# Equal start addresses modulo 512 bytes for every tile that TensorE reads

## The chip, the cores and the metric

The kernel runs on one NeuronCore of a Trainium2 chip. The metric is the device time of one execution in microseconds (us). All arrays are float32. Matrix products are made in float32 with three products per pair of operands (below), so TensorE does three times the work of the plain formula.

## The reference, cut to what matters

One encoder layer with shared weights, applied to a prompt of 256 tokens and a sample of 1024 tokens, width 1024:

```python
def encoder_layer(x, mem, ...):
    h = rmsnorm(x, g_mix_pre)
    z = h @ w_in                                     # 1024 -> 9216 columns
    rq, rk, rv, rg, pin, mq, gl = jnp.split(z, ...)
    gates = jax.nn.sigmoid(gl).reshape(b, s, 3, 1024)
    y_ret = retention_branch(rq, rk, rv, rg, ...) @ w_ret_out   # 4 heads, both directions, chunks
    y_pool = pool_branch(pin, pool_w, pool_scale) @ w_pool_out
    y_mem = memory_branch(mq, mem, g_mem, w_mem_kv) @ w_mem_out # 256 memory tokens, softmax
    merged = gates[:, :, 0] * y_ret + gates[:, :, 1] * y_pool + gates[:, :, 2] * y_mem
    x = x + rmsnorm(merged @ w_o, g_mix_post)
    h2 = rmsnorm(x, g_ffn_pre)
    u = conv3(h2 @ w_up)                             # 1024 -> 2 * 2816, depthwise conv of width 3
    gate, val = jnp.split(u, 2, axis=-1)
    return x + rmsnorm((gelu(gate) * val) @ w_down, g_ffn_post)
```

## The kernel before

**Work and order.** Tokens of both groups lie side by side (T = 1280). Each operand of a product is split by `hilo` (L136) into a rounded high part (ScalarE, L138 or L141) and the rest (VectorE, L139 or L142), and `mm3` (L145 to L148) makes three matmuls of them into one PSUM bank: high by high (L146), high by low (L147), low by high (L148). The order on every engine is that of the code; nothing reorders it. The stages follow each other: memory keys and values, queries of the memory branch and retention values, the pooling branch with the rotary products, the retention gate with the state chain, the gates with the retention chain, the three output projections, the output product with `w_o`, the feed-forward up product in 22 units with the convolution, and the down product in two halves of 640 tokens.

**What a matmul reads.** Each matmul instruction loads its own stationary operand (128 columns, 512 bytes in each partition; row "LDWEIGHTS" of the profile, engine PEld) and then streams its moving operand of 512 or 256 columns (2048 or 1024 bytes). The load of the next matmul starts while the matmul before it streams. So at any time two places in SBUF are read: the moving tile of the current matmul and the stationary tile of the next.

**Where the tiles lie.** Pools are laid out by hand-chosen order, from the left end of SBUF and, for the weight ring, from the right end.
- `wh` and `wl` (L79, L80): the split weights, four buffers of 4096 bytes each, at the right end.
- `b` (slots of `big`, L121 to L134): eight buffers of `SLOT` = 2·2·642 elements = 10272 bytes = 20·512 + 32, from the left. They hold the split activations hT, the operands of the output projections, five half-terms each of the up product (`hterm`, L1166), and at the end raw down-product input.
- `hc` (L1257): a tile at the right side below the ring, for the last 16 of the 56 half-terms (products B22 and T4).
- `h2p` (L1248): split prompt tokens of the up product, moving operand with 256 columns. `gl` (L1592): split down-product input, stationary. `lh` (L1145): stationary in the `w_o` product. `bx` (L974): two more slots at the right.
- `khl`, `qhl`, `vhl`, `pt` (memory branch), `k1hl`, `v1hl` (states), `qkvhl`, `sthl`, `shl` (retention), `memT` (memory), `pwh`, `dh` (pooling).

In the built program before, the start addresses modulo 512 are: `wh`, `wl` and `hc` 480; the eight buffers of `b` 192, 224, 256, 288, 320, 352, 384, 416; `bx` 416 and 448; `lh` 416; `gl` 256; `h2p` 128; `memT`, `khl`, `qhl`, `vhl`, `k1hl`, `v1hl`, `qkvhl`, `sthl` 128; `pt` 256; `shl` 352; `pwh` 0; `dh` 192 and 320; `ident` 128. Slices that a matmul takes of a tile start at multiples of 512 bytes from the tile's start, except in `dh`.

**The up product** of one unit q (a block of 128 gate columns and 128 value columns) has seven products of 12 matmuls with 512 columns, for the sample (`product`, L1305, matmul at L1309): B11, B21, T2, T1, T3 read half-terms in `b`; B22 and T4 read half-terms in `hc`. All seven take their stationary operand from `wh` and `wl`. Between them stand four groups of 12 matmuls with 256 columns for the prompt (`prompt`, L1312), whose moving operand is `h2p`.

**Small statistics.** Row sums, maxima and reciprocal square roots are tiles of 4 to 64 bytes, allocated in the pool of the stage that uses them.

Of the kernel before, what the change touches and what calls it, by code (L numbers as in the profile page):

```python
# [8 lines left out]
F32 = mybir.dt.float32  # L9
# [3 lines left out]
ALU = mybir.AluOpType  # L13
# [4 lines left out]
P = 128  # L18
# [3 lines left out]
T = TP + TS  # L22
KC = D // P
NT = T // P
H = 4
HD = 256
# [9 lines left out]
PAD = 16  # L36
PW = PAD + TP + PAD + TS + PAD
PCOLS = PW - 2 * PAD
SLOT = 2 * 2 * 642

PK = {}
_o = 0
# [67 lines left out]
def encoder(ctx: ExitStack, tc: tile.TileContext, a: dict):  # L110
    nc = tc.nc

    const = ctx.enter_context(tc.tile_pool(name="const", bufs=1))
    dram = ctx.enter_context(tc.tile_pool(name="scratch", bufs=1, space=DRAM))
    wpool = ctx.enter_context(tc.tile_pool(name="w", bufs=1, side="right"))
    big = ctx.enter_context(tc.tile_pool(name="big", bufs=1))
    ctx.enter_context(tc.manual_schedule())
# [46 lines left out]

    def rsqrt_act(pool, v, between=None):
        s = pool.tile([P, 1], F32, tag="rqs", name="rqs")
        y = pool.tile([P, 1], F32, tag="rqy", name="rqy", bufs=2)
        t = pool.tile([P, 1], F32, tag="rqt", name="rqt")
        nc.scalar.activation(s, v, AF.Sqrt)
        if between:  # L170
            between()
        nc.vector.reciprocal(out=y, in_=s[:])
        nc.vector.tensor_tensor(out=t, in0=y[:], in1=y[:], op=ALU.mult)
        nc.vector.scalar_tensor_tensor(out=t, in0=t[:], scalar=-0.5, in1=v, op0=ALU.mult, op1=ALU.mult)
        nc.vector.scalar_tensor_tensor(out=y, in0=t[:], scalar=1.5, in1=y[:], op0=ALU.add, op1=ALU.mult)
        return y
# [34 lines left out]
    nc.scalar.activation(warm, ident[:, 0:1], AF.Exp)  # L211
    pk = const.tile([P, PK_W], F32, name="pk")
    kc = const.tile([P, KC_W], F32, name="kc")

    def col(name, i=0, n=1):
        o, _ = PK[name]
# [69 lines left out]
    dec = ds.enter_context(tc.tile_pool(name="dec", bufs=1))  # L286
# [17 lines left out]
    b = chb(512)  # L304
# [81 lines left out]
            if c not in (4, 6):  # L386
                yield

    lg = dec.tile([P, 2 * H], F32, name="lg")
    kdec = dec.tile([P, 2, H, 2], F32, name="kdec")  # L390
    qdec = dec.tile([P, 2, H, 2], F32, name="qdec")
    cdec = dec.tile([P, 2 * H], F32, name="cdec")
    dtab = dec.tile([P, H, 2, C], F32, name="dtab")

    def decay_tables():
        d = col("decay_fwd", 0, 2 * H)
        u, s, s2, r = (s0.tile([P, 2 * H], F32, name=f"lg{i}") for i in range(4))
        nc.vector.tensor_scalar(out=u, in0=d, scalar1=-1.0, scalar2=None, op0=ALU.mult)
        nc.vector.tensor_tensor(out=u, in0=u[:], in1=d, op=ALU.min)
        nc.scalar.activation(u, u[:], AF.Exp)  # L400
        nc.vector.tensor_scalar(out=s, in0=u[:], scalar1=2.0, scalar2=None, op0=ALU.add)
        nc.vector.reciprocal(out=s, in_=s[:])
        nc.vector.tensor_tensor(out=s, in0=s[:], in1=u[:], op=ALU.mult)
        nc.vector.tensor_tensor(out=s2, in0=s[:], in1=s[:], op=ALU.mult)
        nc.vector.tensor_scalar(out=r, in0=s2[:], scalar1=2.0 / 19, scalar2=2.0 / 17, op0=ALU.mult, op1=ALU.add)
        for k in range(7, -1, -1):
            nc.vector.tensor_tensor(out=r, in0=r[:], in1=s2[:], op=ALU.mult)
            nc.vector.tensor_scalar(out=r, in0=r[:], scalar1=2.0 / (2 * k + 1), scalar2=None, op0=ALU.add)
        nc.vector.tensor_tensor(out=r, in0=r[:], in1=s[:], op=ALU.mult)
        nc.vector.tensor_scalar(out=u, in0=d, scalar1=0.0, scalar2=None, op0=ALU.min)  # L410
        nc.vector.tensor_tensor(out=lg, in0=u[:], in1=r[:], op=ALU.subtract)
        yield
        nc.scalar.activation(cdec, lg[:], AF.Exp, scale=float(C))
        for h in range(H):
            for dr in range(2):
                sc = lg[:, dr * H + h:dr * H + h + 1]
                nc.scalar.activation(qdec[:, dr, h, :], kcol("cmi" if dr else "ip1"), AF.Exp, scale=sc)
                nc.scalar.activation(kdec[:, dr, h, :], kcol("j" if dr else "cm1j"), AF.Exp, scale=sc)
        kd = kdec[:].rearrange("p a b c -> p (a b c)")
        nc.vector.tensor_scalar(out=kd, in0=kd, scalar1=HD ** -0.5, scalar2=None, op0=ALU.mult)  # L420
        yield
        rel = s0.tile([P, 2, 2 * C], F32, name="rel")
        nc.sync.dma_start(out=rel, in_=a["rel"])
        for h in range(H):
            dt = dtab[:, h].rearrange("p a b -> p (a b)")
            nc.vector.tensor_scalar(out=dt, in0=rel[:, 0, :], scalar1=lg[:, h:h + 1], scalar2=None, op0=ALU.mult)
            nc.vector.scalar_tensor_tensor(out=dt, in0=rel[:, 1, :], scalar=lg[:, H + h:H + h + 1], in1=dt,
                                           op0=ALU.mult, op1=ALU.add)
            nc.scalar.activation(dt, dt, AF.Exp)
            nc.vector.tensor_scalar(out=dt, in0=dt, scalar1=HD ** -0.5, scalar2=None, op0=ALU.mult)  # L430
            yield
# [67 lines left out]
    def mem_chain():  # L499
# [28 lines left out]
        def scores(n):  # L528
            h, j = jobs[n]
            q, k, mo = qs.pop(n), khl[h], (MEM if j else 0)  # L530
            b = chb(2, MEM)
            for i in range(2):
                for d in range(2):
                    ts = slice(i * P, (i + 1) * P)
                    mm3(b[:, i, :], q[:, 0, d, ts], q[:, 1, d, ts],
                        k[:, 0, d, mo:mo + MEM], k[:, 1, d, mo:mo + MEM], d == 0, d == 1)
            mx = mp.tile([P, 2], F32, tag="mx", name="mx", bufs=2)
            sm = mp.tile([P, 2], F32, tag="sm", name="sm", bufs=2)
            e = pr[n] = mp.tile([P, 2, MEM], F32, tag="pr", name="pr", bufs=2)
            nc.vector.tensor_reduce(out=mx, in_=b, axis=AX.X, op=ALU.max)  # L540
            nc.vector.tensor_scalar(out=mx, in0=mx[:], scalar1=-(HD ** -0.5), scalar2=None, op0=ALU.mult)
            for i in range(2):
                nc.scalar.activation(e[:, i, :], b[:, i, :], AF.Exp, scale=HD ** -0.5, bias=mx[:, i:i + 1],
                                     accum_out=sm[:, i:i + 1])
            nc.vector.reciprocal(out=sm, in_=sm[:])
            for i in range(2):
                nc.vector.tensor_scalar(out=e[:, i, :], in0=e[:, i, :], scalar1=sm[:, i:i + 1], scalar2=None,
                                        op0=ALU.mult)
# [34 lines left out]
        t = 0  # L583
# [249 lines left out]
    def ret_chain(rp):  # L833
# [51 lines left out]
        def output(n):  # L885
# [10 lines left out]
            if drs:  # L896
# [4 lines left out]
                for i in range(2):  # L901
# [5 lines left out]
                    for dr in drs:  # L907
                        nc.vector.scalar_tensor_tensor(out=y[:, i, :], in0=b[:, dr - lo, :],
                                                       scalar=qdec[:, dr, h, i:i + 1], in1=y[:, i, :],
                                                       op0=ALU.mult, op1=ALU.add)  # L910
            bs = rp.tile([P, 2, 6], F32, tag="bs", name="bs")
            ag = rp.tile([P, 2, 2], F32, tag="ag", name="ag")
            for i in range(2):
                nc.vector.bn_stats(out=bs[:, i, :], in_=src[:, i, :])
                nc.vector.bn_aggr(out=ag[:, i, :], in_=bs[:, i, :])
            rs = rsqrt(rp, ag[:, :, 1], 2, 1.0)
            for i in range(2):
                nc.vector.tensor_scalar(out=y[:, i, :], in0=src[:, i, :], scalar1=ag[:, i, 0:1],
                                        scalar2=rs[:, i:i + 1], op0=ALU.subtract, op1=ALU.mult)
# [182 lines left out]
    def finish(t, bs, x, bank):  # L1102
        u = xtile()
        v = xtile()
        ss = op.tile([P, 3], F32, tag="ss", name="ss", bufs=2)
        for i in range(2):
            nc.vector.tensor_tensor(out=u[:, i * 512:(i + 1) * 512], in0=bs[i], in1=gpost[:, i * 512:(i + 1) * 512],
                                    op=ALU.mult)
# [1 line left out]
        yield  # L1110
        nc.vector.scalar_tensor_tensor(out=ss[:, 0:1], in0=ss[:, 0:1], scalar=EPS, in1=ss[:, 1:2],
                                       op0=ALU.add, op1=ALU.add)
        rs = rsqrt_act(op, ss[:, 0:1])
        yield
        nc.vector.scalar_tensor_tensor(out=x, in0=u[:], scalar=rs[:, 0:1], in1=x[:], op0=ALU.mult, op1=ALU.add)
        nc.gpsimd.dma_start(out=x2_d[t][:], in_=x[:])
# [1 line left out]
        nc.scalar.activation(v, x[:], AF.Square, scale=D ** -0.5, accum_out=ss[:, 2:3])  # L1118
        yield
        nc.vector.tensor_scalar(out=ss[:, 2:3], in0=ss[:, 2:3], scalar1=EPS, scalar2=None, op0=ALU.add)  # L1120
        r2 = rsqrt_act(op, ss[:, 2:3])
        yield
        nc.vector.tensor_scalar(out=v, in0=x[:], scalar1=r2[:, 0:1], scalar2=None, op0=ALU.mult)
        yield
# [429 lines left out]
    def last_gain(i, hf, b, res):  # L1554
        cs = slice(hf * 512, (hf + 1) * 512)
        nc.vector.tensor_tensor(out=res[i][:, cs], in0=b, in1=gpost2[0][:, cs], op=ALU.mult)
# [27 lines left out]
    for hb in range(2):  # L1584
# [20 lines left out]
                g_split(k)  # L1605
        if hb == 0:
            gpost2.append(gain(a["g_ffn_post"]))
        ss = fp.tile([P, 2, 5], F32, tag="fss", name="fss", bufs=2)
        res = [fp.tile([P, D], F32, tag=f"res{i}", name="res") for i in range(5)]
        bs = [fbank()[:] for _ in range(5)]  # L1610
        held = []
# [34 lines left out]
        for i in range(5):  # L1646
            for n, w in held:
                partial(i, n, w)
            last_half(i, 1, bs[i], res, ss)
            if not hb:  # L1650
                last_gain(i, 1, bs[i], res)
            else:
                v = ss[:, 0, i:i + 1]
                nc.vector.scalar_tensor_tensor(out=v, in0=v, scalar=EPS, in1=ss[:, 1, i:i + 1],
                                               op0=ALU.add, op1=ALU.add)
                rs = rsqrt_act(fp, v, lambda: last_gain(i, 1, bs[i], res))
                close_tile(5 + i, res[i], rs[:, 0:1], xs.pop(0))
                if i + 3 < 5:
                    xs.append(load_x2(5 + i + 3))
# [83 lines left out]
```

## Time and profile before

| what | value |
|---|---|
| time, median of 3 runs | 2740.58 us (2740.44 to 2741.98) |
| profiled execution, its own time | 2741.42 us |
| its span in the profile | 2739.7 us |
| TensorE busy | 2683.1 us, 98% of the span |
| VectorE, ScalarE, GpSimd busy | 50%, 33%, 10% of the span |
| share of TensorE in the chain that ended last | 92% |
| granted TensorE clock, mean | 0.992 of full speed |

A matmul's own duration in the profile overlaps with the next one's. What a matmul costs is the time from its start to the start of the next; a run of equal matmuls gives it as the time from the first start to the start of what follows, divided by their number.

### The profile page before, as it was taken

The numbers are of one execution on the slowest core, as the hardware profiler recorded it, in microseconds if no ns is written. First come the engines' busy times: TensorE is split into PE (matmuls) and PEld (weight loads), VectorE is DVE, ScalarE is ACT, GpSimd is POOL, SyncE is SP. The second block draws the span as 40 slices with busy tenths as digits, with TensorE's granted clock in tenths as the row PEclk, the third lists the DMA queues.
The fourth block names the chain that finished last, engine by engine and source line by source line (L and its number), as shares of the span: only waits on it lengthen the run. The fifth ranks groups of instructions, "written<-read, shape, count | busy, mean of one in ns | idle before, by whom it ended". The sixth has DMA issues, their size and how long they took to land.

```text
span 2739.7 us, 36294 instructions
## 1 busy us (share of the span) xinstructions
PE 2683.1 (98%) x14396; PEld 2293.2 (84%) x14396; DVE 1358.0 (50%) x2281; ACT 910.0 (33%) x1551; POOL 283.8 (10%) x463
## 2 busy tenths in 40 slices
PE   8999999999999999999999999987999999999998
PEld 6988998888888888888888888866888888878776
DVE  5645303446445355555324344655665666554454
ACT  5433312221024233333302121653444344434333
POOL 1111221211123111111100000110000000000000
PEclk9999999999999999999999999998999999999999
DMA  7775466664568444444425343452333333353443
GB/s 254 257 191 141 137 158 160 168 151 117 150 172 219 148 155 153 146 148 145 164 87 164 118 133 114 152 190 85 114 109 109 109 111 111 125 186 119 141 149 108
DMA packets 145595, 401.77 MB, mean 147 GB/s; under 512 B 17712, under 2 KB 27056, under 8 KB 145072
## 3 DMA queue, kind: packets, MB, share of 16 engines
q1 hardware_dynamic: 99808, 269.64, 30.3%
q0 software_dynamic: 45328, 129.53, 17.2%
q8 instruction: 113, 1.85, 0.3%
q14 instruction: 58, 0.48, 0.1%
q10 hardware_dynamic: 288, 0.28, 0.0%
HBM read 306.32 MB, written 144.97 MB: 165 GB/s over the span
## 4 chain that ended last, share of the span: by engine, by line
PE 92%; DVE 2%; DMA 2%; ACT 2%; issue 1%; SPq 0%; POOL 0%; DVEq 0%; ACTq 0%; POOLq 0%
PE f L1309 15%; PE mm L148 13%; PE mm L146 13%; PE mm L147 13%; PE f L148 10%; PE f L146 10%; PE f L147 10%; PE ch L148 3%; PE ch L146 3%; PE ch L147 3%; DMA wr<-w_kv_in 1%; DVE wl L87 0%; DMA x<-x2d 0%; ACT wh L86 0%; PE ch L555 0%
## 5 line engine op out<-in xcount | busy, mean ns | idle before, releaser
L148 PE MATMUL mm<-b,wl 128*128 128x512 f32 (+1 forms) x1536 | 550.0, 358 | 0.0
L146 PE MATMUL mm<-b,wh 128*128 128x512 f32 (+1 forms) x1536 | 548.3, 357 | 0.0
L147 PE MATMUL mm<-b,wh 128*128 128x512 f32 (+1 forms) x1536 | 546.1, 356 | 0.0
L87 DVE TENSOR_TENSOR wl<-wr,wh 128x1024 fp32r<-128x1024 f32 x244 | 297.6, 1223 | 421.6 <-ACT wh L86 417.3
L86 ACT ACTIVATE wh<-wr 128x1024 fp32r<-128x1024 f32 x244 | 255.2, 1050 | 293.7 <-PE f L147 153.1
L147 PEld LDWEIGHTS mm<-b,wh 128*128 128x128 f32 x1536 | 288.9, 188 | 45.5
L148 PEld LDWEIGHTS mm<-b,wl 128*128 128x128 f32 x1536 | 288.7, 188 | 45.1
L146 PEld LDWEIGHTS mm<-b,wh 128*128 128x128 f32 x1536 | 288.7, 188 | 42.7
L1309 PE MATMUL f<-b,wh 128*128 128x512 f32 x880 | 279.7, 399 | 8.5 <-ACT b L138 7.2
L1309 PEld LDWEIGHTS f<-b,wh 128*128 128x128 f32 x880 | 162.7, 190 | 43.9 <-ACT b L138 8.1
L1309 PE MATMUL f<-b,wl 128*128 128x512 f32 x440 | 175.0, 398 | 0.0
L148 PE MATMUL f<-wh,gl 128*128 128x512 f32 x390 | 155.9, 400 | 4.6 <-DVE gl L139 4.5
L146 PE MATMUL f<-wh,gl 128*128 128x512 f32 x390 | 155.6, 399 | 1.5 <-ACT gl L138 1.5
L147 PE MATMUL f<-wl,gl 128*128 128x512 f32 x390 | 155.4, 398 | 0.0
L148 PE MATMUL f<-b,wl 128*128 128x512 f32 (+1 forms) x432 | 154.3, 357 | 0.0
L146 PE MATMUL f<-b,wh 128*128 128x512 f32 (+1 forms) x432 | 154.0, 356 | 0.0
L147 PE MATMUL f<-b,wh 128*128 128x512 f32 (+1 forms) x432 | 153.5, 355 | 0.0
L139 DVE TENSOR_TENSOR gl<-b,gl 128x640 fp32r<-128x640 f32 x78 | 64.0, 825 | 122.8 <-ACT gl L138 122.8
L146 PE MATMUL f<-h2p,wh 128*128 128x256 f32 x352 | 101.7, 289 | 15.6 <-ACT h2p L138 5.8
L138 ACT ACTIVATE gl<-b 128x640 fp32r<-128x640 f32 x78 | 57.1, 738 | 165.2 <-PE f L148 156.2
L960 ACT ACTIVATE gate<-mm 128x512 f32<-128x512 f32 (+1 forms) x68 | 35.6, 524 | 227.9 <-PE mm L148 135.9
L1309 PE MATMUL f<-hc,wh 128*128 128x512 f32 x352 | 109.3, 392 | 0.0
(344 smaller groups left out, 5299.6 us busy)
## 6 DMA issues: line engine op xcount, KB each, us to landing
wr<-w_in_in SPq DMA_DIRECT2D x72, 512.0 KB, 4.1
wr<-w_up_in SPq DMA_DIRECT2D x44, 512.0 KB, 3.6
wr<-w_down_in SPq DMA_DIRECT2D x44, 512.0 KB, 3.6
b<-fgd SPq DMA_DIRECT2D x44, 320.0 KB, 4.8
h2s<-gtd SPq DMA_DIRECT2D x48, 256.0 KB, 3.8
s12d<-w_up_in SPq DMA_DIRECT2D x22, 512.0 KB, 6.7
s34d<-w_up_in SPq DMA_DIRECT2D x22, 512.0 KB, 7.5
s12d<-w_up_in POOLq DMA_DIRECT2D x22, 512.0 KB, 7.6
```

The lines of the kernel that those rows point to most:

```text
L86: self.nc.scalar.activation(h, r[:], AF.Copy)
L87: self.nc.vector.tensor_tensor(out=l, in0=r[:], in1=h.bitcast(F32), op=ALU.subtract)
L138: nc.scalar.activation(hi, src, AF.Copy)
L139: nc.vector.tensor_tensor(out=lo, in0=src, in1=hi.bitcast(F32), op=ALU.subtract)
L146: nc.tensor.matmul(out, ah, bh, start=first, stop=False)
L147: nc.tensor.matmul(out, ah, bl, start=False, stop=False)
L148: nc.tensor.matmul(out, al, bh, start=False, stop=last)
L960: nc.scalar.activation(y[:, 0:n], b, AF.Sigmoid)
L1309: nc.tensor.matmul(b, w[x][:, ks], hterm(nm, c, y), start=first and c == k == 0, stop=last and c == 3 and k == 2, skip_group_check=True)
```

## The change

No instruction is added, removed or moved: both built programs hold the same instructions in the same order with the same semaphore waits on every engine. What differs is where tiles lie. `SLOT` becomes 2·1280 elements = 10240 bytes = 20·512. Small tiles move into a pool `tiny` that is laid out once ahead of `big`, and an unused tile of 16 elements fills up. Two small tiles grow (`fss` to 512 bytes, the reciprocal root to two elements).

```diff
-SLOT = 2 * 2 * 642
+SLOT = 2 * T
...
+    tiny = ctx.enter_context(tc.tile_pool(name="tiny", bufs=1))
     wpool = ctx.enter_context(tc.tile_pool(name="w", bufs=1, side="right"))
     big = ctx.enter_context(tc.tile_pool(name="big", bufs=1))
...
-        y = pool.tile([P, 1], F32, tag="rqy", name="rqy", bufs=2)
+        y = pool.tile([P, 2], F32, tag="rqy", name="rqy", bufs=2)[:, 0:1]
...
+    const.tile([P, 16], F32, name="pad")
...
-    lg = dec.tile([P, 2 * H], F32, name="lg")
-    kdec = dec.tile([P, 2, H, 2], F32, name="kdec")
+    lg = tiny.tile([P, 2 * H], F32, name="lg")
+    kdec = tiny.tile([P, 2, H, 2], F32, name="kdec")
...
-            mx = mp.tile([P, 2], F32, tag="mx", name="mx", bufs=2)
-            sm = mp.tile([P, 2], F32, tag="sm", name="sm", bufs=2)
+            mx = tiny.tile([P, 3], F32, tag="ss", name="mx", bufs=2)
+            sm = tiny.tile([P, 2], F32, tag="rqy", name="sm", bufs=2)
...
-            rs = rsqrt(rp, ag[:, :, 1], 2, 1.0)
+            rs = rsqrt(tiny, ag[:, :, 1], 2, 1.0)
...
-        ss = op.tile([P, 3], F32, tag="ss", name="ss", bufs=2)
+        ss = tiny.tile([P, 3], F32, tag="ss", name="ss", bufs=2)
...
-        ss = fp.tile([P, 2, 5], F32, tag="fss", name="fss", bufs=2)
+        ss = fp.tile([P, P], F32, tag="fss", name="fss", bufs=2)[:, 0:10].rearrange("p (a b) -> p a b", b=5)
```

In the built program after, `wh`, `wl`, `hc`, all of `b` and `bx`, `lh`, `gl`, `h2p`, `memT` and the tiles of the memory branch, the states and retention start at 480 modulo 512. Only `pwh` (352), `dh` (32 and 160) and `ident` (128) differ. Call a matmul equal when its moving slice and its stationary slice start at the same address modulo 512. The two programs hold, counted from their addresses:

| matmuls | before, equal | before, unequal | after, equal | after, unequal |
|---|---|---|---|---|
| 512 columns | 684 | 7668 | 8256 | 96 |
| 256 columns | 816 | 4896 | 5664 | 48 |
| 128 columns (transposes) | 158 | 174 | 14 | 318 |

## Rows read from the trace of the kernel before

**Rows 1.** The page: busy time by engine, and the chain by engine.
```profile
PE 2683.1 (98%) x14396; PEld 2293.2 (84%) x14396; DVE 1358.0 (50%) x2281; ACT 910.0 (33%) x1551; POOL 283.8 (10%) x463
...
PE 92%; DVE 2%; DMA 2%; ACT 2%; issue 1%; SPq 0%; POOL 0%; DVEq 0%; ACTq 0%; POOLq 0%
```

**Rows 2.** Windows: length, busy us (instructions) by engine, clock, DMA share, GB/s.
```profile
1800.00:1900.00 100.00, 72.47 (x313) 58.32 (x313) 61.10 (x113) 45.57 (x96) 6.71 (x10) 0.85 0.41 133
...
2100.00:2300.00 200.00, 200.00 (x1053) 170.90 (x1053) 120.19 (x137) 85.77 (x112) 8.62 (x16) 1.00 0.33 111
```

**Rows 3.** The chain, up product, about one unit: start us, us, what.
```profile
2098.83 5.53 PE f L1309 x24
...
2105.78 5.55 PE f L1309 x24
...
2112.76 2.73 PE f L1309 x12
...
2116.92 5.62 PE f L1309 x24
```

**Rows 4.** Timeline of PE, the same unit: start us, us of one.
```profile
2105.62 0.62 PE L1309 MATMUL f<-b,wh 128*128 128x512 f32 x2
...
2108.40 0.63 PE L1309 MATMUL f<-hc,wh 128*128 128x512 f32 x2
...
2111.17 0.28 PE L146 MATMUL f<-h2p,wh 128*128 128x256 f32 x1
...
2112.59 0.63 PE L1309 MATMUL f<-hc,wh 128*128 128x512 f32 x2
...
2115.33 0.28 PE L146 MATMUL f<-h2p,wh 128*128 128x256 f32 x1
```

**Rows 5.** Timeline of PE, gates with the retention chain.
```profile
943.16 0.28 PE L146 MATMUL ch<-qkvhl 128*128 128x256 f32 x1
...
944.58 0.39 PE L146 MATMUL mm<-b,wh 128*128 128x512 f32 x1
...
950.17 0.28 PE L146 MATMUL ch<-qkvhl,sthl 128*128 128x256 f32 x1
...
951.59 0.28 PE L146 MATMUL mm<-b,wh 128*128 128x256 f32 x1
...
954.43 0.40 PE L146 MATMUL mm<-b,wh 128*128 128x512 f32 x1
```

**Rows 6.** Timeline of PE, state chain.
```profile
863.72 0.39 PE L146 MATMUL ch<-v1hl,k1hl 128*128 128x512 f32 x1
...
866.03 0.39 PE L147 MATMUL ch<-v1hl,k1hl 128*128 128x512 f32 x1
```

**Rows 7.** Timeline of PE, down product.
```profile
2520.38 0.40 PE L146 MATMUL f<-wh,gl 128*128 128x512 f32 x1
...
2524.58 0.40 PE L146 MATMUL f<-wh,gl 128*128 128x512 f32 x1
```

**Rows 8.** PE groups by form: busy us, mean ns | idle before.
```profile
L148 PE MATMUL mm<-b,wl 128*128 128x512 f32 x1024 | 406.4, 397 | 0.0
...
L1309 PE MATMUL f<-b,wh 128*128 128x512 f32 x880 | 279.7, 399 | 8.5 <-ACT b L138 7.2 <-DVE b L139 1.2
L1309 PE MATMUL f<-b,wl 128*128 128x512 f32 x440 | 175.0, 398 | 0.0
L148 PE MATMUL f<-wh,gl 128*128 128x512 f32 x390 | 155.9, 400 | 4.6 <-DVE gl L139 4.5
...
L148 PE MATMUL f<-b,wl 128*128 128x512 f32 x288 | 114.0, 396 | 0.0
...
L1309 PE MATMUL f<-hc,wh 128*128 128x512 f32 x352 | 109.3, 392 | 0.0
```

More of the change, by code (lines that the diff above doesn't have):

```diff
@@ L172, in rsqrt_act @@
         nc.vector.reciprocal(out=y, in_=s[:])
-        nc.vector.tensor_tensor(out=t, in0=y[:], in1=y[:], op=ALU.mult)
+        nc.vector.tensor_tensor(out=t, in0=y, in1=y, op=ALU.mult)
         nc.vector.scalar_tensor_tensor(out=t, in0=t[:], scalar=-0.5, in1=v, op0=ALU.mult, op1=ALU.mult)
@@ L387, in x_stats @@
                 yield
-    lg = dec.tile([P, 2 * H], F32, name="lg")
-    kdec = dec.tile([P, 2, H, 2], F32, name="kdec")
-    qdec = dec.tile([P, 2, H, 2], F32, name="qdec")
-    cdec = dec.tile([P, 2 * H], F32, name="cdec")
+    lg = tiny.tile([P, 2 * H], F32, name="lg")
+    kdec = tiny.tile([P, 2, H, 2], F32, name="kdec")
+    qdec = tiny.tile([P, 2, H, 2], F32, name="qdec")
+    cdec = tiny.tile([P, 2 * H], F32, name="cdec")
     dtab = dec.tile([P, H, 2, C], F32, name="dtab")
@@ L396, in decay_tables @@
         d = col("decay_fwd", 0, 2 * H)
-        u, s, s2, r = (s0.tile([P, 2 * H], F32, name=f"lg{i}") for i in range(4))
+        u, s, s2, r = (tiny.tile([P, 2 * H], F32, name=f"lg{i}") for i in range(4))
         nc.vector.tensor_scalar(out=u, in0=d, scalar1=-1.0, scalar2=None, op0=ALU.mult)
@@ L536, in scores @@
                         k[:, 0, d, mo:mo + MEM], k[:, 1, d, mo:mo + MEM], d == 0, d == 1)
-            mx = mp.tile([P, 2], F32, tag="mx", name="mx", bufs=2)
-            sm = mp.tile([P, 2], F32, tag="sm", name="sm", bufs=2)
+            mx = tiny.tile([P, 3], F32, tag="ss", name="mx", bufs=2)
+            sm = tiny.tile([P, 2], F32, tag="rqy", name="sm", bufs=2)
             e = pr[n] = mp.tile([P, 2, MEM], F32, tag="pr", name="pr", bufs=2)
+            mx = mx[:, 0:2]
             nc.vector.tensor_reduce(out=mx, in_=b, axis=AX.X, op=ALU.max)
-            nc.vector.tensor_scalar(out=mx, in0=mx[:], scalar1=-(HD ** -0.5), scalar2=None, op0=ALU.mult)
+            nc.vector.tensor_scalar(out=mx, in0=mx, scalar1=-(HD ** -0.5), scalar2=None, op0=ALU.mult)
             for i in range(2):
@@ L910, in output @@
                                                        op0=ALU.mult, op1=ALU.add)
-            bs = rp.tile([P, 2, 6], F32, tag="bs", name="bs")
-            ag = rp.tile([P, 2, 2], F32, tag="ag", name="ag")
+            bs = tiny.tile([P, 2, 6], F32, tag="bs", name="bs")
+            ag = tiny.tile([P, 2, 2], F32, tag="ag", name="ag")
             for i in range(2):
@@ L1112, in finish @@
                                        op0=ALU.add, op1=ALU.add)
-        rs = rsqrt_act(op, ss[:, 0:1])
+        rs = rsqrt_act(tiny, ss[:, 0:1])
         yield
@@ L1120, in finish @@
         nc.vector.tensor_scalar(out=ss[:, 2:3], in0=ss[:, 2:3], scalar1=EPS, scalar2=None, op0=ALU.add)
-        r2 = rsqrt_act(op, ss[:, 2:3])
+        r2 = rsqrt_act(tiny, ss[:, 2:3])
         yield
@@ L1655, in encoder @@
                                                op0=ALU.add, op1=ALU.add)
-                rs = rsqrt_act(fp, v, lambda: last_gain(i, 1, bs[i], res))
+                rs = rsqrt_act(tiny, v, lambda: last_gain(i, 1, bs[i], res))
                 close_tile(5 + i, res[i], rs[:, 0:1], xs.pop(0))
```

## The prediction

> **What bounds the kernel now.** I began with the page's busy times and its chain: TensorE is busy for 2683.1 of 2739.7 us and holds 92% of the chain that ended last [rows 1]. The reader is to see that only two things can move the time: the 56.6 us in which TensorE idles, and the spacing of 14396 matmuls. Next the windows by stage. Where the work is steady, 2100 to 2300 us, TensorE is busy without a gap; the large hole lies between 1800 and 1900 us, where 27.5 us are lost at the passage from the output product to the up product [rows 2]. That hole is a chain of ScalarE, VectorE and DMA work, which the change leaves as it is.
>
> So the question is whether a matmul's spacing depends on where its operands lie. The chain through one unit of the up product answers it: runs of 24 matmuls that are the same instruction in the same line take 5.53, 5.55 and 5.62 us, and one of 12 takes 2.73 us [rows 3]. There is no wait in them, the clock is at full speed (1.00, the 2.4 GHz level) and the other engines do the same work in each unit [rows 2]. What differs between the runs is which tile streams. By the order of the code the 5.53 us run is T3 and T1, both in `b`; the 5.62 us run is B21 and T2, both in `b`; the 5.55 us run is B11 in `b` followed by B22 in `hc`; the 2.73 us run is T4 in `hc`.
>
> **The change part by part.**
>
> *Instructions and waits.* None is added, removed or moved, and no wait changes. The move of the small tiles into their own pool, the two tiles that grow and the unused pad therefore cost nothing and win nothing by themselves; they serve the addresses. VectorE, ScalarE and DMA also see other addresses, all still multiples of 32 bytes. Each of the three holds 2% of the chain [rows 1]; their work lies under that of TensorE elsewhere. I take 0 for them, with 2 us either way (1 to 2% of some 160 us of chain).
>
> *512 columns, unequal before.* Three places give the spacing now. In the up product the five products from `b` take 5.53 + 5.62 us, and B11 from 2105.62 to 2108.40, 2.78 us [rows 3, 4]: 13.93 us for 60 matmuls, 232.2 ns each. In the gates, 24 matmuls stand from 944.58 to 950.17 us: 5.59 us, 232.9 ns each [rows 5]. In the down product 18 stand from 2520.38 to 2524.58 us: 4.20 us, 233.3 ns each [rows 7]. The gates have the most of them (groups of 1024 in each of three lines) beside 1320 in the up product and 390 in each of three lines in the down product [rows 8]. I take 232.7 ns.
>
> *512 columns, equal.* The trace already holds such matmuls. The two `hc` products run from 2108.40 to 2111.17 and from 2112.59 to 2115.33 us [rows 4]: 5.51 us for 24, 229.6 ns each; by the chain, 5.55 + 2.73 − 2.78 = 5.50 us, 229.2 ns [rows 3]. This is the best comparison there is: same line, same weights, same unit, a few microseconds apart. A second place is the state chain, whose tiles all start at 128: 10 matmuls from 863.72 to 866.03 us, 2.31 us, 231.0 ns each [rows 6]. It is a smaller sample at another address, so I weigh `hc` about ten to one, by the number of matmuls, and take 229.5 ns. The difference is 3.2 ns. For 7668 matmuls that become equal: −24.5 us. Bounds from the same rows: with T4 alone, 2.73 us for 12 or 227.5 ns, −5.2 ns each and −40 us; with the state chain alone, −1.7 ns each and −13 us.
>
> *256 columns.* Equal ones are in the retention chain: 12 from 943.16 to 944.58 us and 12 from 950.17 to 951.59 us, both 1.42 us, 118.3 ns each. Unequal ones in the gates: 24 from 951.59 to 954.43 us, 2.84 us, 118.3 ns [rows 5]. With `h2p` in the up product, 12 from 2111.17 to 2112.59 us, 1.42 us, 118.3 ns again [rows 4]. Here equality shows nothing, so there is no gain to claim: I take +0.3 ns (the resolution of such a reading is about 0.5 ns) for 4896, +1.5 us, and from −1 to +1 ns, −5 to +5 us, as bounds. Why the short ones don't answer I can't see from the trace; it makes the mechanism less certain than the sizes.
>
> *Transposes and the pooling.* 144 of the 158 equal transposes become unequal; at the largest difference that these rows show between two places, 5 ns, that is 0.7 us, and I take 0. The 144 matmuls of the pooling branch stay unequal.
>
> *Sum.* −24.5 + 1.5 = −23 us, against a profiled execution of 2741.42 us (span 2739.7 us) that lies 0.8 us over the median of 2740.58 us; I subtract from the median: 2717.6, say **2718 us**, −0.8%. The steady stages scale with it evenly, since no other engine is near its limit there: VectorE is busy 120 of 200 us [rows 2].
>
> **A rule against the change.** The rows say that spacing varies by 1 to 2% with the streamed tile and nothing else. The Trainium skill, page "TensorE: Matmul & The Clock Gate", Part 2, step 1, says that TensorE has two independent SBUF read ports and that loading the next weights takes no read bandwidth from the running matmul. By that rule no address could matter and the change would give nothing. The trace does not agree for whole products: 5.53 against 5.62 us for the same 24 instructions, without a wait [rows 3].
>
> **The rivals.**
>
> *It does nothing (2741 us).* The load of the next weights and the stream of the moving tile don't meet at all, or meet by something other than equality modulo 512, for instance by higher address bits, and the average over many pairs stays 232.7 ns: 7668 times 0. For it: the two `hc` products, both equal, differ by 0.03 us in 12 [rows 4], unequal pairs reach 5.53/24 = 230.4 ns, nearly as low [rows 3], and the 256-column ones show no effect. Against it: both places with equal tiles lie under the average of the unequal ones around them, and `hc` does so in one and the same unit. Chance 0.09. The Trainium skill's rule on the two read ports ("TensorE: Matmul & The Clock Gate", Part 2) leads here; the trace agrees only in the 256-column runs.
>
> *Slower (2755 us).* After the change all eight slots are alike not only modulo 512 but modulo 2048 (10240 = 5·2048), so whatever a pair meets, all pairs meet; before, eight different offsets averaged it out. If the good `hc` figure comes from its place at the right end and equal pairs from the left behave like the worst run seen, 5.62/24 = 234.2 ns [rows 3], then 7668 · (234.2 − 232.7) = +11.5 us, and with +1 ns on the short ones +5 us more: up to 2757, centre 2755. It decides from 233.4 ns on (+5.5 us). Against it: weights are taken in steps of 512 bytes, so every product runs through all four places modulo 2048, and both equal places that the trace has are under the average. Chance 0.07.
>
> *A smaller gain (2731 us).* Equal pairs settle at the state chain's 231.0 ns [rows 6] and the short ones lose 1 ns: −13 + 5 = −8 us, up to −10. It lies on the forecast's side and inside its range.
>
> *Another engine becomes the bound.* TensorE's 200 us of the steady stage would have to shrink to VectorE's 120 [rows 2]. Excluded.
>
> **How the numbers follow.** Faster by at least 0.2% (5.5 us, about what a measurement of this kernel can tell from no change): the forecast with the smaller gain, 0.84. Within 0.2%: 0.09. Slower: 0.07. The low end is the −40 us bound shaded for the short ones, 2702; the high end is the smaller gain with the 2 us for the holes, 2735. Outside lie most of the 0.16 of the other two cases.
>
> **What would show it.** In the chain of the changed kernel the runs of 24 in the up product should all be near 5.50 us, and the 24 matmuls of a gate group near 5.51 us where they took 5.59; the 18 of the down product near 4.13 us. Groups of 12 with `h2p` should stay at 1.42 us, `hc` at 2.77 and 2.73 us, since these pairs don't change. The hole of 27.5 us after 1800 us should keep its length and come some 15 us earlier. I am wrong if 512-column runs from `b` keep their spread, or if they agree at 5.6 us; I am wrong in size if the short ones move by more than 1 ns either way.

## The result, and the profile after

| | time, median (lowest to highest) | runs |
|---|---|---|
| before, same chip | 2741.28 us (2740.44 to 2742.78) | 4 |
| after | 2709.61 us (2707.08 to 2710.93) | 4 |

The ratio is 0.9883 [0.9866, 0.9900]: 31.7 us less. The profiled execution took 2709.01 us, its span is 2707.2 us and its mean clock 0.991. The page of the changed kernel, where [rows 1] stood before:

```profile
PE 2650.3 (98%) x14396; PEld 2298.8 (85%) x14396; DVE 1358.4 (50%) x2281; ACT 910.0 (34%) x1551; POOL 283.7 (10%) x463
...
PE 93%; DVE 2%; DMA 2%; ACT 2%; issue 1%; SPq 0%; POOL 0%; DVEq 0%; ACTq 0%; POOLq 0%
```

Everything that was won is TensorE's busy time: 32.8 us less for the same 14396 matmuls, with VectorE and ScalarE where they were. The hole and the steady stage, by windows, beside [rows 2]:

```profile
1780.00:1880.00 100.00, 72.34 (x316) 58.64 (x316) 61.53 (x117) 46.16 (x99) 6.71 (x10) 0.85 0.42 136
2100.00:2300.00 200.00, 200.00 (x1064) 172.99 (x1063) 121.37 (x137) 86.73 (x115) 8.62 (x16) 1.00 0.34 112
```

The hole keeps its length (27.7 us against 27.5) and lies some 20 us earlier. In the steady 200 us, at the same clock, 1064 matmuls begin where 1053 did. The chain through the up product, beside [rows 3]:

```profile
2070.21 5.47 PE f L1312 x24
...
2077.11 5.47 PE f L1312 x24
...
2084.01 5.47 PE f L1312 x24
...
2090.91 2.75 PE f L1312 x12
```

The spread is gone: the third row is B11 in `b` with B22 in `hc`, and it takes what two products from `b` take. Single places, by the timeline of PE: the gate group behind the state chain's transposes, a gate group with the retention chain beside [rows 5], the `hc` products beside [rows 4] and the down product beside [rows 7]:

```profile
859.33 0.60 PE L768 MATMUL ch<-ident,k 128*128 128x128 f32 x4
859.69 0.48 PE L147 MATMUL mm<-b,wh 128*128 128x512 f32 x1
860.00 0.40 PE L148 MATMUL mm<-b,wh 128*128 128x512 f32 x1
...
865.25 0.39 PE L147 MATMUL ch<-v1hl,k1hl 128*128 128x512 f32 x1
...
936.59 0.40 PE L147 MATMUL mm<-b,wh 128*128 128x512 f32 x1
...
942.05 0.28 PE L147 MATMUL ch<-qkvhl,sthl 128*128 128x256 f32 x1
...
943.49 0.28 PE L147 MATMUL mm<-b,wh 128*128 128x256 f32 x1
...
946.37 0.40 PE L147 MATMUL mm<-b,wh 128*128 128x512 f32 x1
...
2086.59 0.61 PE L1312 MATMUL f<-hc,wh 128*128 128x512 f32 x2
...
2089.31 0.28 PE L147 MATMUL f<-h2p,wh 128*128 128x256 f32 x1
...
2090.74 0.63 PE L1312 MATMUL f<-hc,wh 128*128 128x512 f32 x2
...
2093.49 0.28 PE L147 MATMUL f<-h2p,wh 128*128 128x256 f32 x1
...
2488.21 0.39 PE L148 MATMUL f<-wl,gl 128*128 128x512 f32 x1
...
2492.29 0.39 PE L148 MATMUL f<-wl,gl 128*128 128x512 f32 x1
```

A gate group of 24 takes 942.05 − 936.59 = 5.46 us (5.59 before), 18 of the down product 4.08 us (4.20 before). The 24 gate matmuls with 256 columns take 2.88 us (2.84 before): they became slower. The `hc` products, whose own addresses did not change, went from 2.77 and 2.74 to 2.72 and 2.75 us. The gate group at 859.69 us, right behind transposes, takes 865.25 − 859.69 = 5.56 us. The same group stood at 866.84 us before:

```profile
866.84 0.48 PE L146 MATMUL mm<-b,wh 128*128 128x512 f32 x1
867.15 0.39 PE L147 MATMUL mm<-b,wh 128*128 128x512 f32 x1
...
872.49 0.39 PE L146 MATMUL ch<-v1hl,k1hl 128*128 128x512 f32 x1
```

It took 5.65 us then, so it gained 0.09 us. Its first matmul takes 0.31 us in both kernels, where other groups begin with 0.23: that is why it is longer than they are, and the change has no part in it.

Both programs hold the same matmuls in the same order, so each matmul's spacing (its start to the next start) can be set beside its own in the other trace; the table's means and sums are worked out from the two traces in this way. Equal is taken here of its moving slice and the stationary slice of the matmul behind it:

| matmuls, without a wait in either trace | number | before, ns | after, ns | sum, us |
|---|---|---|---|---|
| 512 columns, newly equal | 7416 | 232.70 | 227.70 | −37.1 |
| 512 columns, equal in both | 684 | 229.41 | 227.79 | −1.1 |
| 256 columns, newly equal | 4773 | 118.25 | 119.68 | +6.8 |
| transposes, all | 309 | | | 0.0 |
| 256 and 512 columns, others | 911 | | | +0.2 |
| spacings that hold a wait | 302 | | | −1.3 |

First to last start shrinks by 32.4 us (2730.9 to 2698.5).

### The profile page after: what moved, and what is told of

The parts are those of the page before. It is cut to its first block, busy times and chain, and to the rows that moved or that the text cites. A ratio compares the mean times of both kernels' runs of the same rounds, so it can differ in the third digit from the quotient of the medians.

```text
span 2707.2 us, 36294 instructions
## 1 busy us (share of the span) xinstructions
PE 2650.3 (98%) x14396; PEld 2298.8 (85%) x14396; DVE 1358.4 (50%) x2281; ACT 910.0 (34%) x1551; POOL 283.7 (10%) x463
## 4 chain that ended last, share of the span: by engine, by line
PE 93%; DVE 2%; DMA 2%; ACT 2%; issue 1%; SPq 0%; POOL 0%; DVEq 0%; ACTq 0%; POOLq 0%
PE f L1312 15%; PE mm L148 13%; PE mm L147 13%; PE mm L149 13%; PE f L149 10%; PE f L148 10%; PE f L147 10%; PE ch L148 3%; PE ch L149 3%; PE ch L147 3%; DMA wr<-w_kv_in 1%; DVE wl L87 0%; DMA x<-x2d 0%; ACT wh L86 0%; PE ch L558 0%
## 5 line engine op out<-in xcount | busy, mean ns | idle before, releaser
L149 PE MATMUL mm<-b,wl 128*128 128x512 f32 (+1 forms) x1536 | 543.7, 354 | 0.0
```

Of the source, the lines that this page charges most:

```text
L149: nc.tensor.matmul(out, al, bh, start=False, stop=last)
```

## The experiments

All are made from the changed kernel. Below, the **distance** of a pair is the address of the moving slice minus that of the stationary slice which the next matmul loads. "Smaller staging" is one buffer fewer in a staging pool of the first stage, to make room. By the traces e3 and e4 run 1.5 and 2.9 us longer than the changed kernel between first and last matmul, 1.3 and 2.8 of it in the first 70 us. Part of that may be the price of the smaller staging; kernels that keep the staging differ there too, by −1.3 (e8) to +0.5 us (e7).

**Everything on the right side 32 bytes lower (e1).** `wh`, `wl`, `hc`, `bx` and `lh` move to 448; `b`, `h2p`, `gl` stay at 480. Pairs from `b` get distance 32, those of the down product −32, `hc` stays equal.

```diff
+    rpad = ctx.enter_context(tc.tile_pool(name="rpad", bufs=1, side="right"))
+    rpad.tile([P, 8], F32, name="rpad")
     wpool = ctx.enter_context(tc.tile_pool(name="w", bufs=1, side="right"))
```

> The right end (weight ring, hc, bx, lh) moves by 32 bytes against the left end; nothing else changes. 7128 matmuls with 512 columns and 4368 with 256 columns become unequal again by 32 bytes, but all left tiles stay alike among themselves, and hc and the ring too. Theory A, equality of the two streams counts: 512-column spacing from b goes back to about 232.7 ns, hc stays at 227.7, 256 columns go back from 119.7 to 118.3 ns; +36 - 6 = +30 us, 2739 us. Rival B, regularity of the moving tiles among themselves counts, not the pair: stays at 2710 us with 227.7 ns. Rival C, the skill's rule that loads take nothing from streams: stays at 2710 us.

Measured: 2740.20 us (2735.49 to 2741.81, 10 runs), 0.9998 [0.9989, 1.0007] of before. The chain in the up product:

```profile
2095.08 5.60 PE f L1314 x24
...
2102.08 5.55 PE f L1314 x24
...
2109.03 2.75 PE f L1314 x12
```

32 bytes take the whole gain back, though the eight slots are still alike among themselves. So regularity by itself does not win (rival B), and it is not true that the two reads have nothing to do with each other (rival C). Nor is it traffic of other engines that happens to fall on some matmuls: in e1, of the 41 runs of 24 from `b` in the up product, 40 repeat the same 24 spacings within 1 ns (the other one stands next to the hole).

**And the left side lower too (e2).** The same pad, and the left one half as large, so that everything is equal again, at 448.

```diff
+    rpad.tile([P, 8], F32, name="rpad")
...
-    const.tile([P, 16], F32, name="pad")
+    const.tile([P, 8], F32, name="pad")
```

> Both ends move by 32 bytes the same way: all tiles that were at 480 modulo 512 are at 448; equality is kept. Theory A and B: same as after, 2710 us, 512 columns at 227.7 ns, 256 columns at 119.7 ns. Rival D, the absolute address 480 counts (a tile that starts 32 bytes under a boundary): another time, by up to the +30 us of the first run.

Measured: 2709.73 us (2708.00 to 2710.61, 4 runs), 0.9885 [0.9869, 0.9902].

```profile
2091.83 2.75 PE f L1314 x12
...
2102.91 5.47 PE f L1314 x24
```

Whether all tiles lie at 480 or at 448 makes no difference; where the moving tile lies against the weights does.

**Right side 256 and 512 bytes lower (e3, e4).** The pad of e1 with 64 and 128 elements, smaller staging.

> The right end moves by 256 bytes (and one staging buffer less in the first 120 us makes room). Theory A with a plain yes or no of equality: 512 columns from b at 232.7 ns, 2739 us. Theory A with a distance that matters: the trace of before has 231.0 ns as the mean of its pairs 256 apart, so 7128 * 3.3 - 6 = +18 us, 2728 us. Rivals B and C: 2710 us.

> The right end moves by 512 bytes, with the same smaller staging: equal modulo 512 again, not modulo 1024 as in after. Theory A with a period of 512: 2710 us, 227.7 ns. Rival E, the period is 1024 or 2048 and after happens to sit well in it: another spacing, by up to the difference of the two hc products of before, 2.5 ns or 19 us. The staging buffer alone may move the first 120 us by at most 2 us.

Measured: e3 2710.69 us (2710.51 to 2711.95, 4 runs), 0.9891 [0.9876, 0.9906]; e4 2711.99 us (2710.32 to 2712.12, 4 runs), 0.9893 [0.9879, 0.9908]. The chain of e3:

```profile
2110.50 5.47 PE f L1314 x24
...
2117.40 2.75 PE f L1314 x12
```

e4 came as expected, e3 did not: 256 bytes are as good as 0. What counts for an equal pair is the distance modulo 256, not 512.

**Right side 64 and 128 bytes lower (e5, e6).** The pad with 16 and 32 elements, smaller staging, to find whether the period is shorter still.

> The right end moves by 64 bytes (with the smaller staging). Two theories of the period are left after the runs at 32, 256 and 512 bytes: F, only multiples of 256 are good: 512 columns from b near 233 ns, about 2739 us. G, the period is 64 bytes: 227.7 ns, 2710 us. In between: the period is 128: as F here and as G in the run at 128.

> The right end moves by 128 bytes (with the smaller staging). F, only multiples of 256 are good: near 233 ns, about 2739 us. G or a period of 128: 227.7 ns, 2710 us.

Measured: e5 2709.41 us (2707.76 to 2711.67, 4 runs), 0.9891 [0.9875, 0.9908]; e6 2740.42 us (2739.27 to 2743.90, 10 runs), 1.0004 [0.9995, 1.0014]. The chain of e5, then of e6:

```profile
2084.38 2.76 PE f L1314 x12
...
2095.42 5.49 PE f L1314 x24
...
2102.27 5.49 PE f L1314 x24
```

```profile
2099.16 5.60 PE f L1314 x24
...
2106.18 5.55 PE f L1314 x24
...
2113.16 2.76 PE f L1314 x12
```

A distance of 64 is nearly as good as 0 for `b`, one of 128 as bad as 32: no single period makes that. So theory G's 2710 us for e5 came true by luck, since e5 is good and bad at once. Its pairs of the down product have distance −64, and they run at 233.3 ns; its time is still low because the 256-column matmuls got shorter. The timeline of PE in e5 shows two groups of 12 with `h2p`:

```profile
2100.75 0.28 PE L149 MATMUL f<-h2p,wh 128*128 128x256 f32 x1
...
2102.11 0.62 PE L1314 MATMUL f<-b,wh 128*128 128x512 f32 x2
...
2107.60 0.28 PE L149 MATMUL f<-h2p,wh 128*128 128x256 f32 x1
...
2109.02 0.40 PE L1314 MATMUL f<-hc,wh 128*128 128x512 f32 x1
```

Behind a product from `b` (distance 64) they take 1.36 us, behind one from `hc` (distance 0) 1.42 us, at the same distance of their own, 64. It is so throughout the up product behind the hole: groups behind `b` take 1.36 us and groups behind `hc` 1.42, whatever follows them.

**Only `h2p` and `gl` moved, by 32 bytes (e7).** With the longer `h2p` tile (in e9 and e10 as well) SyncE also has one wait instruction fewer, where `h2p` is loaded, so these three are compared stage by stage.

```diff
-            h2p = up.tile([P, KC, 2, TP], F32R, name="h2p")
+            h2p = up.tile([P, KC * 2 * TP + 8], F32R, name="h2p")[:, 8:].rearrange("p (a b c) -> p a b c", b=2, c=TP)
...
-                g = fp.tile([P, 2, 640], F32R, tag="gl", name="gl", bufs=3)[:]
+                g = fp.tile([P, 2 * 640 + P], F32R, tag="gl", name="gl", bufs=3)[:, 8:1288].rearrange("p (a b) -> p a b", b=640)
```

> From after, two tiles alone start 32 bytes later: h2p (moving, 256 columns, up product) and gl (stationary, 512 columns, down product). Theory A: the down product goes from 226.8 to 233 ns, 1170 * 6 = +7 us, and nothing else of 512 columns moves; h2p goes from 119.3 to about 117 ns as in the first run, 1056 * -2.3 = -2.4 us. Sum +4.6 us, 2714 us. Rival: the loss of 256 columns at equality has to do with the 512-column products before them, then h2p stays at 119.3 ns.

Measured: 2712.52 us (2709.79 to 2713.07, 4 runs), 0.9901 [0.9886, 0.9916]. A group with `h2p` in its timeline:

```profile
2101.78 0.28 PE L147 MATMUL f<-h2p,wh 128*128 128x256 f32 x1
...
2103.19 0.63 PE L1312 MATMUL f<-b,wh 128*128 128x512 f32 x2
```

Each part does what the whole of e1 does there: `h2p` at 32 shortens its group to 1.41 us (1.42 to 1.43 in the changed kernel), by the traces 2.1 us less between 1900 and 2300 us; `gl` at −32 costs 6.4 us from 2420 us on.

**The two `hc` products moved (e8).** B22 by 16 bytes, T4 by 192.

```diff
-            return hslots[8][:, i - 40, :]
+            o = (i - 40) * HS + (4 if i < 48 else 48)
+            return hslots[8][:, o:o + HS]
...
-    hslots.append(hc.tile([P, 16, HS], F32R, name="hc"))
+    hslots.append(hc.tile([P, 16 * HS + P], F32R, name="hc"))
```

> From after, hc alone is displaced inside: the half-terms of B22 by 16 bytes, those of T4 by 192. Products from b stay at 2.72 and 2.75 us. F: both hc products go to 2.80 us (233 ns). G (64 or 128): T4 stays at 2.72 to 2.75 us. For B22 at 16 bytes theory A says 2.80 us if any distance inside the period loses, 2.73 us if distances under 32 bytes are free.

Measured: 2712.32 us in one run. Its chain:

```profile
2096.62 5.47 PE f L1313 x24
...
2110.42 5.53 PE f L1313 x24
...
2117.38 2.81 PE f L1313 x12
```

The 5.53 us run holds B22, at some 2.78 us; T4 takes 2.81. Both lose (231.5 and 233.8 ns in the trace, where equal ones take 227.7): 16 bytes are already too many, and 192 (that is −64) is as bad for a stream from `hc` as −64 was for the down product.

**`h2p` at 64 (e9), and the other short ones as well (e10).** If 64 suits 256 columns better, take it for these alone and leave 512 columns at 0. In e10 `khl`, `pt`, `v1hl`, the queries and values of `qkvhl` move by 64 bytes as well, and `shl` by 128.

```diff
-            h2p = up.tile([P, KC, 2, TP], F32R, name="h2p")
+            h2p = up.tile([P, KC * 2 * TP + 16], F32R, name="h2p")[:, 16:].rearrange("p (a b c) -> p a b c", b=2, c=TP)
```

> From after, h2p alone starts 64 bytes later. In the run at 64 bytes groups of 12 with h2p took 1.36 us behind a product from b and 1.42 behind one from hc, against 1.43 in after. Theory H, the best distance is 0 for 512 and 64 for 256 columns: 1.36 us, 1056 * -6 = -6 us, 2703 us. Rival: the 1.36 us came from the products before it, which stood at 64 bytes too; then 1.40 to 1.43 us and 2707 to 2710 us.

> As the run before, and the moving tiles of the other separate 256-column products (khl, pt, v1hl, the q and v parts of qkvhl, shl) 64 bytes past their stationary tiles too; 1056 + 1152 matmuls with 256 columns and 192 with 512 columns at 64 bytes. Theory H: -6 us of h2p and 1152 * -4 = -4.5 us more, 2699 us. Rival: as there, 2705 us or more; the retention and memory groups are short and stand among 512-column products.

Measured: e9 2709.55 us (2709.05 to 2712.97, 4 runs), 0.9889 [0.9874, 0.9903]; e10 2711.79 us (2710.91 to 2712.29, 4 runs), 0.9894 [0.9879, 0.9909]. The timeline of e9:

```profile
2100.64 0.28 PE L147 MATMUL f<-h2p,wh 128*128 128x256 f32 x1
...
2102.05 0.63 PE L1312 MATMUL f<-b,wh 128*128 128x512 f32 x2
```

Theory H misses both times. At 64 behind a product at distance 0 the group takes 1.41 us, not e5's 1.36. So e5 owed the 1.36 to the products ahead, which also ran at 64. In e10 the other short pairs went from 119.2 to 120.0 ns down to 117.8 to 118.1, and the 512-column pairs that moved with them from 227.9 to 229.0 up to 231.1 to 231.4. Its trace is 3.0 us longer than the changed kernel's, most of it in the hole (2.0 us) and between 2400 and 2600 us (2.1 us), where no tile was moved; why, is open.

**`SLOT` back to what it was (e11).** The rest of the change stays, so the eight slots of `b` again start 32 bytes apart, smaller staging.

```diff
-SLOT = 2 * T
+SLOT = 2 * 2 * 642
```

> From after, SLOT alone goes back to 10272 bytes (with the smaller staging): the slots of b start at 0, 32, 64, ... 224 past 480 and all that lies behind them is displaced by 256 in all, which the run at 256 bytes found free. Theory A with the distances measured so far (0 and 64 good, the rest near 233 ns): about 4000 matmuls with 512 columns lose 5.4 ns and 660 lose 1.5, the short ones win 2 us: +20 us, 2730 us. If SLOT were not the main part: under 2718 us.

Measured: 2736.39 us (2733.85 to 2738.28, 10 runs), 0.9987 [0.9977, 0.9996]. Its chain:

```profile
2097.37 5.58 PE f L1312 x24
...
2104.38 5.54 PE f L1312 x24
...
2111.35 2.75 PE f L1312 x12
```

By the traces it runs 24.8 us longer than the changed kernel: `SLOT` is the bulk of the change, more than expected. In e11 pairs that stream from `b` average 231.7 ns at distance 0 and 232.5 at 64, where all-equal streams have 227.7 and e5's steady 64 has 229.2. A good slot among bad ones loses most of its advantage. With `gl` and `hc` still equal, the down product is as fast as in the changed kernel (0.0 us by the trace).

**e5 with `gl` equal again (e12).** Distance 64 for `b` and `h2p`, 0 for the down product.

```diff
+    rpad.tile([P, 16], F32, name="rpad")
...
-                g = fp.tile([P, 2, 640], F32R, tag="gl", name="gl", bufs=3)[:]
+                g = fp.tile([P, 2 * 640 + P], F32R, tag="gl", name="gl", bufs=3)[:, 112:1392].rearrange("p (a b) -> p a b", b=640)
```

> The run at 64 bytes once more, with gl (stationary of the down product) moved along with the weights, so that it is equal again. In the trace of the run at 64 bytes the stages from 70 to 600 us were 8.8 us shorter than in after, mostly where 256-column products stand alone at 64 or -64 bytes, and the down product 9.1 us longer. If distances act stage by stage, only the 9 us go: 2709.4 - 9 = 2700 us, 0.3% under after. If what the run at 64 bytes won was compensated by something that follows, it stays at 2709 us.

Measured: 2704.14 us (2701.53 to 2708.41, 4 runs), 0.9874 [0.9856, 0.9892]. A stretch of the down product, by windows of PE alone, in the changed kernel, e5 and e12 (length, busy us, matmuls begun, clock, DMA share, GB/s):

```profile
2420.00:2550.00 130.00, 128.41 (x565) 1.00 0.36 121
```

```profile
2420.00:2550.00 130.00, 128.42 (x549) 1.00 0.34 112
```

```profile
2420.00:2550.00 130.00, 128.41 (x559) 0.99 0.35 113
```

`gl` wins back 5.5 of the 9.1 us that e5 lost from 2420 us on; some 140 pairs there whose stationary slice lies in `b` stay at −64 and at 233 ns. The stages from 70 to 600 us are 8.8 us shorter than in the changed kernel, as in e5, so distances act stage by stage. By the traces e12 is 5.5 us shorter than the changed kernel, but the two ratio intervals overlap: that it beats the changed kernel is likely and not shown by the times.

The spacing by distance, worked out as in the table above (mean over all pairs of the kind, without waits, the first ones behind another tile or width included):

| distance modulo 256 | 512 columns, ns | 256 columns, ns |
|---|---|---|
| 0, nearly all pairs equal (after, e3) | 227.6 to 227.7 | 119.6 to 119.7 |
| 0, among unequal ones (e1, e5, e6) | 229.5 to 229.9 | 118.9 to 119.3 |
| 16 (e8) | 231.5 | |
| 32 (e1) | 233.3 | 117.1 |
| −32 (e1) | 233.3 | 118.3 |
| 64 (e5) | 229.2 | 115.9 |
| −64 (e5) | 233.3 | 113.8 |
| 128 (e6) | 232.8 | 118.7 to 118.9 |

## Why the prediction was right in direction and short in size

**That spacing depends on where the operands lie, and on nothing else that the change does: shown.** e1 takes away the whole gain by moving addresses alone and e2 gives it back. The rival "it does nothing" falls. The Trainium skill ("TensorE: Matmul & The Clock Gate", Part 2, step 1) gives TensorE two independent SBUF read ports, one for each operand. What the prediction drew from that, that no address could matter, does not agree with these runs: 32 bytes between the two operands are the 30.5 us from e2 to e1. The 256-column runs, in which the prediction saw the rule confirmed, depend on the distance too.

**That it is equality modulo 512: too narrow.** The period is 256 (e3), and 64 in one direction serves 512 columns nearly as well as 0 (e5, e12) while −64 does not. The unequal 5.53 us run from `b` [rows 3], which the rival held against me, is of this kind: by the addresses, 7 of its 24 pairs were at distance 0 modulo 256 already and 7 at 64, and of the 5.62 us run none.

**"I weigh `hc` about ten to one ... and take 229.5 ns": the term that was mis-sized.** It measured 227.7 ns, −37.1 us instead of −24.5. The sample was twelve matmuls long, and an equal stream does not reach its spacing at once. T4 and the end of B22 in the kernel before, beside [rows 4]:

```profile
2110.49 0.62 PE L1309 MATMUL f<-hc,wh 128*128 128x512 f32 x2
...
2113.29 0.62 PE L1309 MATMUL f<-hc,wh 128*128 128x512 f32 x2
```

B22, behind an unequal product, takes 2.09 us for its first nine matmuls (232 ns each) and 0.68 for the last three (227); T4, behind `h2p`, 0.70 us for the first three (about 232) and 2.04 for the other nine (227). The settled 227 ns stood in the trace, and the mean over whole products mixed it with the way there. T4 of the changed kernel, from 2090.74 us:

```profile
2092.13 0.61 PE L1312 MATMUL f<-hc,wh 128*128 128x512 f32 x2
```

It needs 1.39 us for the first six (231 ns each) and 1.36 for the last six (227), while B22, now behind an equal product, is settled from its first matmul on. So what the change adds is that few equal pairs are left unsettled: of those at distance 0, 82% stand at 226 to 228 ns in the changed kernel, 29% before. The 684 pairs that were equal already went from 229.4 to 227.8 ns without an edit of their own; e1, e5 and e6 put equal pairs back among unequal ones and read 229.5 to 229.9. The bound from T4 alone, 227.5 ns, was nearer because T4 happened to settle early.

**256 columns, "+0.3 ns": mis-sized the other way.** They went from 118.25 to 119.68 ns, +6.8 us where I had +1.5 with 5 us as the bound, and past the 1 ns by which I had said that I would be wrong in size. With 256 columns equality is a loss: each other distance in the table is shorter. The instances that the prediction read could hardly show it: before, 256-column pairs at distance 0 averaged 118.7 ns, and the others 117.0 to 118.9. And `h2p` hid it, since its group moved by only 0.01 us.

**Pools, small tiles, transposes at 0: held.** VectorE and ScalarE kept their times, the hole its length, transposes 0.0 us. The sum: 12.6 us more from the long term, 5.3 less from the short one, 1.1 more from pairs already equal and 1.3 from spacings with waits, which I had not counted, 0.2 less from the others: 9.5 us beyond the −23, against 32.4 − 23 = 9.4 in the profiled execution. That the time fell well inside the range owes something to luck: the two mis-sized terms partly cancel. The hole came 20 us earlier where I had 15, for the same reason.

**"Slower", since all pairs meet alike modulo 2048: fell.** Equal pairs from `b` settle at 227 ns, not at 234, and e4, which moves the weights by 512 bytes against `b`, changes nothing after the first stages.

**Open.** What in the chip makes 0 and 64 good and ±32, 128 and −64 bad was not found; no run here separates the reading of SBUF from what TensorE does with it. Nor do they tell whether the moving slice meets the stationary slice of its own matmul or that of the next one: in nearly all runs of matmuls the two lie at the same address modulo 256.

## What to carry to other kernels

Where long runs of matmuls have no waits between them, read the spacing by operand tile before anything else: here the same instruction at 5.47 or 5.60 us per 24 was worth 31 us, and a pad of 32 bytes decided it. Take the price of a state from a stretch that is wholly in that state: look at the single starts, and leave out the first ones behind another tile or width. And price short and long streams apart, since what serves 512 columns can cost with 256.

## What the runs showed of the hardware that was not expected

- Spacing depends on the signed distance modulo 256 between the moving slice and the stationary slice (the next one's, as counted here), not monotonically: with 512 columns 227.7 ns at 0, 231.5 at 16, 233.3 at 32, 229.2 at 64, 232.8 at 128, 233.3 at −64.
- With 256 columns the order is another: 119.6 ns at 0, 117.1 at 32, 115.9 at 64, 113.8 at −64.
- Spacing depends on what ran ahead. With 512 columns at distance 0 the first three (T4 before) to nine matmuls (B22 before) behind another tile or width take 224 to 236 ns, and then each takes 227. With 256 columns 12 matmuls at distance 64 take 1.36 or 1.42 us, all 12 evenly, by what ran ahead (e5, e9). What resets such a state was not tried.
- Behind four transposes the first matmul with 512 columns takes 0.31 to 0.32 us where it takes 0.23 behind other matmuls, before and after alike: the ten gate groups of 24 that stand there take 5.57 us in the changed kernel (5.65 to 5.68 before), the others 5.44 to 5.47.
